# One encoder layer on one core: first rows, gate units, head turns and the first chunks of w_down put in another order

## The chip, the core and the metric

The kernel runs as one program on one core of one Trainium2 chip. The metric is the device time of one execution in microseconds (us); lower is better. The input is one sequence of 512 tokens with 1024 channels, all in float32. Three executions of the kernel before took 872.28, 873.8 and 875.06 us; their median, 873.8 us, is the time that the changed kernel is held against.

## The reference

```python
n = rms_norm(h, mix_norm_g)
proj = n @ w_in                                  # 5120 columns: xa | zu | zv | ga | gb
ya = s5_branch(xa, ...)                          # bidirectional state-space scan, then a GLU
yb = sgu_branch(zu, zv, ...)                     # gating within 128-token chunks
merged = sigmoid(ga) * (ya @ w_proj_a) + sigmoid(gb) * (yb @ w_proj_b)
h = h + merged @ w_out
h = h + memory_cross_attention(rms_norm(h), rms_norm(mem), w_q, w_k, w_v, w_xo)   # 4 heads of 256
h = h + (silu(rms_norm(h) @ w_gate) * (rms_norm(h) @ w_up)) @ w_down              # 2816 wide
return rms_norm(h, final_norm_g)
```

## The kernel before, in words

**Products.** TensorE (PE) is fed float32 numbers as two parts: `split` (L83) copies a tile to a rounded "hi" on ScalarE (ACT, L85) and takes the remainder "lo" on VectorE (DVE, L86). Each product is then three matmuls, hi by hi, hi by lo and lo by hi (`mm3`, L390). A weight tile is 128 x 1024 numbers. It is loaded into one of three `wraw` buffers by SyncE's DMA queue (SP), split into one of three `whi` and three `wlo` buffers, and used. Large products (gates of `b`, queries, feed-forward) are done by a Strassen-Winograd scheme: seven smaller products `q` = 1 to 7 for each "unit" of 512 columns, with sums of operands made by DVE or by accumulating DMAs.

**Order.** The list `plan` (L329 to L362) names every weight tile in the order of use; `next_w` (L365) issues loads some entries ahead and splits up to two entries ahead. `tick` (L485) counts the planned PE time in steps of 5.2 us and starts what `later` (L475) has put down as due; the state-space branch (S5) is a generator, `s5_program`, that `tick` feeds in between. The order in which the lines are traced gives priorities only: when the program is built, a scheduler places each engine's instructions by its own model of their times, so an instruction that it takes to be ready can be hoisted over ones traced before it. At run time each engine works through its queue in the order so fixed. `keep_in_program_order` (`in_order`) pins an instruction against the other pinned ones of its engine; `tc.issue_after(ins)` puts the instructions traced in its block behind `ins` on that engine.

**First rows.** The token tiles are called t = 0 to 3 (128 rows each, `xt`). Each is squared and summed on ACT (L515), its factor is made by two small DVE instructions and one on GpSimd (POOL, L524 to L526), it is scaled on DVE, turned by eight PE transposes (`ptr`, L554) and split into `xn_hi`, `xn_lo`. In `first_rows` (L607) the gain row is spread over the partitions by small matmuls into `pg`; ACT copies it to `g_mix` (L615) and DVE scales tile 0 straight from `pg` (L616). The first use is `tokm(w_in, OFF_V, ...)` (L1095): for each of four weight tiles, six matmuls into the bank `pt` of each of four token tiles; tiles 0 and 1 go token by token as they come, tiles 2 and 3 at the end.

**S5.** `s5_setup` loads `s5_log_step` into a column of `slab` (L684) and takes its exponential on ACT (L726). `s5_kernels(o)` (L832) makes the products `pk` one tick later (L900). `s5_outputs(p)` (L988) copies the states `zh` into `ss` on ACT (L1002, L1003) and makes the products `py` on PE (L1015); the second pass is traced from tick 34 on (L1065). The four 128 x 1024 tiles `gw` of the b gates stand in the place of `zh` (tag `zh`, L1275), so their loads (L242) wait for the copies.

**b's gates.** `ORDER` (L224) is the order of the two units i = 0, 1 of the gate `b`; `gate_step` (L1306) does one product (24 matmuls of 128 x 256).

**Heads.** `scores` (L1491) makes the softmax of a head, `turn_probs` (L1515) turns it by PE transposes `ppt` and splits it, `values` (L1525) makes the head's output: two groups `po` of six matmuls, each in a bank that ACT and DVE then split into `ot_hi`, `ot_lo`. Heads are counted 0 to 3 in the code. `tokm(w_xo, 0, ...)` (L1598) multiplies the outputs by the first half of w_xo: its weight tiles 0 and 1 need heads 0 and 1, tiles 2 and 3 need heads 2 and 3. Head 2 is turned ahead of it, head 3 one tick into it, and the `hook` makes both heads' values after the blocks of tiles 0 and 1.

**w_down.** `plan_units` (L266) and the loop at L1755 hold the order of the ten feed-forward units. In the last one the first two of six chunks of `down_product(dx, 1, ...)` (L1774) stand between products 6 and 7; `x` is copied to `u3` on ACT (L1776) after product 7, and product 4 goes onto the same bank.

Of the kernel before, what the change touches and what calls it, by code (L numbers as in the profile page):

```python
# [17 lines left out]
P = 128  # L18
# [34 lines left out]
def hybrid_layer_kernel(  # L53
# [29 lines left out]
    def split(dst_hi, dst_lo, src):  # L83

        hi = nc.scalar.copy(dst_hi, src)  # L85
        lo = nc.vector.tensor_tensor(dst_lo, src, dst_hi.bitcast(F32), ALU.subtract)  # L86
        if pinned[0]:
            in_order(hi)
            in_order(lo)


    pinned = [False]
# [131 lines left out]
    ORDER = ((1, 0), (2, 0), (5, 0), (6, 0), (1, 1), (7, 0), (2, 1), (5, 1), (6, 1), (3, 0), (7, 1), (4, 0), (4, 1), (3, 1))  # L224
# [41 lines left out]
    def plan_units(units, down):  # L266
# [122 lines left out]

    def mm3(ps, a, b, start, stop, free=False):  # L390

        for i, (x, y) in enumerate(((0, 0), (0, 1), (1, 0))):
            nc.tensor.matmul(ps, a[x], b[y], start=start and i == 0, stop=stop and i == 2, skip_group_check=free)  # L393
# [38 lines left out]
    def tokm(w, c0, act, nk, evac, ntok=NT, last=2, kpt=2, hook=None, cut=None, t0=0):  # L432
# [6 lines left out]
        for wi in range(nw):  # L439
# [4 lines left out]
            if wi < nw - last:  # L444
# [6 lines left out]
                tick(1.3 * ntok)  # L451
        for t in toks:
# [5 lines left out]
            else:  # L458
                tok_block(ps[t], t, held, act, kpt, full, nw == last, True)
# [88 lines left out]
    def to_feat(src, hi, lo, tsl, full=None, skip=None, part=(0, 1), behind=None):  # L548

        for q in part:  # L550
            ps = aux("ptr", (P, 4, P))
            for j in range(4):
                k = 4 * q + j
                tr = nc.tensor.transpose(ps[:, j, :], src[:, k * P:(k + 1) * P], ident)  # L554
                if behind is not None:
                    in_order(tr)
            if q != skip:
                split(hi[:, 4 * q:4 * q + 4, tsl], lo[:, 4 * q:4 * q + 4, tsl], ps)
# [48 lines left out]
    def first_rows():  # L607
# [4 lines left out]
        idles(2)  # L612
        r = rms_factor(row_sums(xt[:, 0, :]))
        for i in range(2):
            in_order(nc.scalar.copy(g_mix[:, HALF[i]], pg[i]))  # L615
            in_order(nc.vector.scalar_tensor_tensor(xt[:, 0, HALF[i]], xt[:, 0, HALF[i]], r, pg[i], ALU.mult, ALU.mult))  # L616
# [12 lines left out]
    for t in range(1, NT):  # L629
        rms_scale(xt[:, t, :], g_mix, xt[:, t, :], ss)  # L630
# [3 lines left out]
        if t == 1:  # L634
            ss3 = row_sums(xt[:, 3, :])
            pinned[0] = False
        if t == 2:
            ss = ss3

# [33 lines left out]
    def s5_setup():  # L673
# [1247 lines left out]
```

## Time and profile before

| what | value |
|---|---|
| executions of the kernel, us | 872.28, 873.8, 875.06 |
| the profiled execution, us | 875.6 |
| its span, first to last instruction, us | 873.8 |
| PE busy, us (share) | 860.3 (98%) |
| DVE busy, us (share) | 648.0 (74%) |
| ACT busy, us (share) | 475.6 (54%) |
| mean granted PE clock | 0.991 |

The profiled execution took 875.6 us, of which 873.8 us lie between its first and its last instruction; 1.8 us lie around them. A busy engine has an instruction in work; as matmuls overlap each other, PE counts as busy also where they come at half their rate. The granted clock says where that is so.

### The profile page before, as it was taken

To read this page: it belongs to the slowest core of one execution; us is meant where nothing else is said; L and a number is where in the kernel's file an instruction comes from. 1 tells how busy PE (TensorE), PEld (TensorE's weight loads), DVE (VectorE), ACT (ScalarE), POOL (GpSimd) and SP (SyncE) were. 2 spreads that over 40 slices of the span, in tenths; PEclk is the share of its full clock that TensorE was granted. 3 is DMA by queue.
4 is the path that set the end of the run, shared out by engine and by line. 5 is a ranking of instruction groups with operands and counts; after the bars stand their busy time and mean duration, and the time that the engine had idled before them with its cause. 6 is when DMAs were issued, how large, how long until landed. Compare 5 with 4: busy or idle time off the path is not lost.

```text
span 873.8 us, 14852 instructions
## 1 busy us (share of the span) xinstructions
PE 860.3 (98%) x5897; PEld 764.8 (88%) x5897; DVE 648.0 (74%) x897; ACT 475.6 (54%) x704; POOL 108.8 (12%) x157
## 2 busy tenths in 40 slices
PE   8999999999999999999999999999999999999996
PEld 6788888878889988889899878999999999888875
DVE  5599679867748768679658656867877778889875
ACT  5453875267436544557547444645545454655663
POOL 1000066100611010110000001001111111000000
PEclk8999999999999999999999999999999999999998
DMA  7457559844647687934688144557799777467672
GB/s 235 121 154 223 115 179 234 203 121 153 173 121 197 162 223 202 287 113 167 204 253 218 54 151 110 145 135 177 173 222 228 201 194 167 135 205 229 197 249 85
DMA packets 110119, 155.40 MB, mean 178 GB/s; under 512 B 8969, under 2 KB 77089, under 8 KB 109986
## 3 DMA queue, kind: packets, MB, share of 16 engines
q1 hardware_dynamic: 91746, 128.27, 45.1%
q0 software_dynamic: 18016, 25.66, 18.5%
q8 instruction: 46, 0.75, 0.3%
q10 hardware_dynamic: 288, 0.52, 0.2%
q14 instruction: 23, 0.19, 0.1%
HBM read 148.70 MB, written 37.20 MB: 213 GB/s over the span
## 4 chain that ended last, share of the span: by engine, by line
PE 95%; DVE 1%; DMA 1%; SPq 1%; ACT 0%; issue 0%; POOLq 0%; POOL 0%; ACTq 0%
PE pf L393 27%; PE pt L393 18%; PE px L1221 12%; PE dx L393 7%; PE pq L1221 6%; PE dq L393 3%; PE pv L1221 3%; PE gx L1221 3%; PE qx L1221 2%; PE dv L393 2%; PE py L1015 1%; DMA slab<-in_s_log_step_dram 1%; PE gq L1221 1%; PE ptr L554 1%; PE po L393 1%; PE qq L1221 1%
## 5 line engine op out<-in xcount | busy, mean ns | idle before, releaser
L86 DVE TENSOR_TENSOR wlo<-wraw,whi 128x1024 fp32r<-128x1024 f32 (+1 forms) x135 | 160.0, 1185 | 82.4 <-ACT whi L85 82.0
L85 ACT CAST whi<-wraw 128x1024 fp32r<-128x1024 f32 (+1 forms) x135 | 138.0, 1023 | 145.0 <-PE pf L393 46.9
L393 PE MATMUL pf<-xn,whi 128*128 128x512 f32 x320 | 100.4, 393 | 0.0
L1221 PE MATMUL px<-fn,whi 128*128 128x256 f32 x480 | 83.3, 276 | 0.0
L1221 PEld LDWEIGHTS px<-fn,whi 128*128 128x128 f32 x480 | 72.5, 188 | 0.3 <-ACT u L1776 0.2
L393 PEld LDWEIGHTS pf<-xn,whi 128*128 128x128 f32 x320 | 59.5, 188 | 12.7 <-issue 0.7
L86 DVE TENSOR_TENSOR wlo<-b,whi 128x1024 fp32r<-128x1024 f32 x40 | 48.9, 1222 | 28.9 <-ACT whi L85 28.9
L85 ACT CAST whi<-b 128x1024 fp32r<-128x1024 f32 x40 | 42.2, 1054 | 51.2 <-PE px L1221 27.1
L1221 PE MATMUL px<-fn,wlo 128*128 128x256 f32 x240 | 66.4, 277 | 0.0
L393 PE MATMUL pf<-xn,wlo 128*128 128x512 f32 x160 | 62.6, 392 | 0.0
L393 PE MATMUL dx<-whi,s 128*128 128x512 f32 x170 | 53.9, 392 | 1.4 <-ACT whi L85 1.0
L1221 PE MATMUL pq<-s,whi 128*128 128x256 f32 x320 | 55.1, 276 | 0.0
L86 DVE TENSOR_TENSOR wlo<-t,whi 128x1024 fp32r<-128x1024 f32 x30 | 36.7, 1224 | 19.9 <-ACT whi L85 19.9
L85 ACT CAST whi<-t 128x1024 fp32r<-128x1024 f32 x30 | 31.6, 1053 | 35.8 <-PE pv L1221 12.6
L1221 PEld LDWEIGHTS pq<-s,whi 128*128 128x128 f32 x320 | 48.3, 188 | 0.1
L393 PE MATMUL pt<-whi,xn 128*128 128x512 f32 x128 | 45.4, 430 | 1.9 <-ACT xn L85 1.9
L1221 PEld LDWEIGHTS px<-fn,wlo 128*128 128x128 f32 x240 | 45.1, 188 | 0.0
L1221 PE MATMUL pq<-s,wlo 128*128 128x256 f32 x160 | 44.2, 277 | 0.0
L393 PEld LDWEIGHTS dx<-whi,s 128*128 128x128 f32 x170 | 31.7, 188 | 8.5 <-ACT whi L85 1.2
L393 PEld LDWEIGHTS pf<-xn,wlo 128*128 128x128 f32 x160 | 30.1, 188 | 6.3 <-issue 0.2
L311 POOL DMA_DIRECT2D dsum<-in_w_down_dram x12 | 13.3, 1108 | 163.3 <-DMA dsum<-in_w_down_dram 163.3
L393 PE MATMUL dx<-wlo,s 128*128 128x512 f32 x85 | 33.1, 390 | 0.0
(478 smaller groups left out, 2342.4 us busy)
## 6 DMA issues: line engine op xcount, KB each, us to landing
wraw<-in_w_in_dram SPq DMA_DIRECT2D x35, 512.0 KB, 5.4
dsum<-in_w_down_dram SPq DMA_DIRECT2D x20, 512.0 KB, 5.7
wraw<-dsum SPq DMA_DIRECT2D x20, 512.0 KB, 3.9
b<-in_w_gate_dram SPq DMA_DIRECT2D x15, 512.0 KB, 4.8
b<-in_w_up_dram SPq DMA_DIRECT2D x15, 512.0 KB, 4.5
wraw<-in_w_down_dram SPq DMA_DIRECT2D x15, 512.0 KB, 4.0
dsum<-in_w_down_dram POOLq DMA_DIRECT2D x10, 512.0 KB, 7.7
dsum<-dsum POOLq DMA_DIRECT2D x10, 512.0 KB, 5.5
```

What stands on the lines that cost most here:

```text
L85: hi = nc.scalar.copy(dst_hi, src)
L86: lo = nc.vector.tensor_tensor(dst_lo, src, dst_hi.bitcast(F32), ALU.subtract)
L311: plan[j + step][1].append((0, lambda d=dst, x=more: nc.gpsimd.dma_start(d, x, accum_op=ALU.add)))
L393: nc.tensor.matmul(ps, a[x], b[y], start=start and i == 0, stop=stop and i == 2, skip_group_check=free)
L554: tr = nc.tensor.transpose(ps[:, j, :], src[:, k * P:(k + 1) * P], ident)
L1015: in_order(nc.tensor.matmul(ps[64 * j:64 * j + 64, :], a, b, start=g % 4 == k == 0, stop=k == 2, tile_position=(0, 64 * j), skip_group_che ...
L1221: nc.tensor.matmul(ps[:, j, :], a[x], b[y], start=start and j == k == i == 0, stop=k == 3 and i == 2, skip_group_check=True)
```

## The change

**First rows.** DVE scales both halves of tile 0 before anything else of `first_rows`; on ACT the hi part of each half of the first weight tile now goes ahead of the copy to `g_mix`; the lo part is pinned behind the lo part of `xn`. Two idle matmul pairs are gone (`idles(2)`). The scaling of tiles 1 to 3 goes behind `xn`'s last lo part, the split of weight tile 2 is traced earlier (its lo part behind tile 1's scaling), and the last `pt` blocks of token tile 0 go behind tile 1's transposes. The exponential of `s5_log_step` goes behind the last hi part of `xn` on ACT, the reduction `rs` (L1136) behind the last lo part on DVE.

**S5 and b.** `pk` of the last two octets is made 1.4 ticks later, not 1; the second pass of `s5_outputs` is traced from tick 36.3; `ORDER` takes products 1 and 2 of both units first.

**Heads.** Head 2 is turned after the first block of w_xo (behind its last matmul), head 3 after the third, values of head 2 after the fifth, of head 3 after the seventh; `tokm` ticks after each block (`fine`).

**w_down.** One chunk stands before product 7 of the last unit, the next one after it.

```diff
-    ORDER = ((1, 0), (2, 0), (5, 0), (6, 0), (1, 1), (7, 0), (2, 1), (5, 1), (6, 1), (3, 0), (7, 1), (4, 0), (4, 1), (3, 1))
+    ORDER = ((1, 0), (1, 1), (2, 0), (2, 1), (5, 0), (6, 0), (5, 1), (7, 0), (6, 1), (3, 0), (7, 1), (4, 0), (4, 1), (3, 1))
...
-            between = [nx[1]] if nx else down[:2]
-            plan.extend([m[5], m[6]] + between + [m[7]] + ([nx[2]] if nx else []) + [m[4], m[3]])
+            between, behind = ([nx[1]], [nx[2]]) if nx else (down[:1], down[1:2])
+            plan.extend([m[5], m[6]] + between + [m[7]] + behind + [m[4], m[3]])
...
+                    if fine:
+                        tick(1.3)
+                if not fine:
+                    tick(1.3 * ntok)
...
-                tok_block(ps[t], t, held, act, kpt, full, nw == last, True)
+                with nullcontext() if behind is None or t > t0 else tc.issue_after(behind):
+                    tok_block(ps[t], t, held, act, kpt, full, nw == last, True)
...
-        idles(2)
         r = rms_factor(row_sums(xt[:, 0, :]))
-        for i in range(2):
-            in_order(nc.scalar.copy(g_mix[:, HALF[i]], pg[i]))
-            in_order(nc.vector.scalar_tensor_tensor(xt[:, 0, HALF[i]], xt[:, 0, HALF[i]], r, pg[i], ALU.mult, ALU.mult))
...
+        for i in range(2):
+            in_order(nc.vector.scalar_tensor_tensor(xt[:, 0, HALF[i]], xt[:, 0, HALF[i]], r, pg[i], ALU.mult, ALU.mult))
         for q in range(2):
-            split(hi[:, q, :], lo[:, q, :], raw[:, q, :])
+            in_order(nc.scalar.copy(hi[:, q, :], raw[:, q, :]))
+            in_order(nc.scalar.copy(g_mix[:, HALF[q]], pg[q]))
             to_feat(xt[:, 0, :], xn_hi, xn_lo, slice(0, P), part=(q,))
+            in_order(nc.vector.tensor_tensor(lo[:, q, :], raw[:, q, :], hi[:, q, :].bitcast(F32), ALU.subtract))
...
-        rms_scale(xt[:, t, :], g_mix, xt[:, t, :], ss)
+        r = rms_factor(ss)
+        with tc.issue_after(turned[1].ins):
+            for i in range(2):
+                scaled = nc.vector.scalar_tensor_tensor(xt[:, t, HALF[i]], xt[:, t, HALF[i]], r, g_mix[:, HALF[i]], ALU.mult, ALU.mult)
...
+            with tc.issue_after(scaled.ins):
+                split_w(2)
+            turned1 = row_tr[0]
...
+        stp = small()
+        with tc.issue_after(last_row[0]):
+            A_.activation(stp, ls, AF.Exp)
...
-        A_.activation(stp, ls, AF.Exp)
...
-        later(1, products)
+        later(1 if o < 2 else 1.4, products)
...
-        while side["now"] < 34:
+        while side["now"] < 36.3:
...
-    tokm(w_in, OFF_V, xn, KD, zv_evac(0))
+    tokm(w_in, OFF_V, xn, KD, zv_evac(0), behind=turned1)
...
-        nc.vector.tensor_reduce(rs, wsr, AX.X, ALU.add)
+        with tc.issue_after(last_row[1]):
+            nc.vector.tensor_reduce(rs, wsr, AX.X, ALU.add)
...
-    turn(2, probs2)
-    later(1, lambda: turn(3, probs3))
+    later(0.2, lambda: turn(2, probs2, last_mm[0].ins))
+    later(0.7, lambda: turn(3, probs3))
+    later(1.2, lambda: values(2, *pts.pop(2)))
+    later(1.7, lambda: values(3, *pts.pop(3)))
...
-    tokm(w_xo, 0, ot, KD, add_evac(0, 1, None), hook=lambda: [values(i, *pts.pop(i)) for i in (2, 3)])
+    tokm(w_xo, 0, ot, KD, add_evac(0, 1, None), fine=True)
...
-            down_product(dx, 1, True, range(2))
+            down_product(dx, 1, True, range(1))
         product(x, u, 7, False, ops)
...
+        else:
+            down_product(dx, 1, True, range(1, 2))
         V.tensor_tensor(u3, q, u3, ALU.subtract)
```

`last_mm`, `turned` and `row_tr` only remember instructions for the `issue_after` blocks; `last_row` holds the hi and lo parts of `xn` made last.

More of the change, by code (lines that the diff above doesn't have):

```diff
@@ L722, in s5_setup @@
         st["c"] = (cr, ci)
-        stp, a, rho, th, n, sn, hs, cs = (small() for _ in range(8))
-        A_.activation(stp, ls, AF.Exp)
+        a, rho, th, n, sn, hs, cs = (small() for _ in range(7))
         V.tensor_tensor(a, lr, stp, ALU.mult)
@@ L1513, in scores, with turn_probs @@
         return prob
-    def turn_probs(hd, prob):
+    def turn_probs(hd, prob, behind=None):
         p_hi = ap_.tile([P, NM, T], F32R, tag="p_hi", name="p_hi", bufs=2)
@@ L1519, in turn_probs @@
             ps = aux("ppt", (P, NT, P))
-            for t in range(NT):
-                nc.tensor.transpose(ps[:, t, :], prob[:, t, mt * P:(mt + 1) * P], ident)
+            with nullcontext() if behind is None else tc.issue_after(behind):
+                for t in range(NT):
+                    nc.tensor.transpose(ps[:, t, :], prob[:, t, mt * P:(mt + 1) * P], ident)
             split(p_hi[:, mt, :], p_lo[:, mt, :], ps.rearrange("p t m -> p (t m)"))
@@ L1541, in hybrid_layer_kernel, with turn @@
     pts = {}
-    def turn(hd, probs):
-        pts[hd] = turn_probs(hd, probs)
+    def turn(hd, probs, behind=None):
+        pts[hd] = turn_probs(hd, probs, behind)
     qx, qq_ = unit_bank("qx"), None
```

16 lines of the change are left out of this document (10 added, 6 removed).

## The prediction

> **What bounds the kernel now.** I read the page first, then PE's waits, the chain, and the timelines of the places named there.
>
> ```profile
> span 873.8 us, 14852 instructions
> PE 860.3 (98%) x5897; PEld 764.8 (88%) x5897; DVE 648.0 (74%) x897; ACT 475.6 (54%) x704; POOL 108.8 (12%) x157
> ```
>
> PE is busy in 860.3 of 873.8 us. The change leaves out only two pairs of idle matmuls, so all it can gain is idle time of PE and time in which PE goes at half clock. From the view of PE's waits (total, times, longest):
>
> ```profile
> PE pt L393 <- ACT xn L85: 1.9, 1, 1.9
> ...
> PE dx L393 <- ACT whi L85: 1.0, 1, 1.0
> PE ppt L1521 <- DVE prob L1512: 0.7, 1, 0.7
> PE pt L393 <- ACT ot_hi L85: 0.7, 1, 0.7
> ...
> ```
>
> These four lie where the change works: xn (first rows), dx behind whi (w_down), ppt and ot_hi (heads); 1.9 + 1.0 + 0.7 + 0.7 = 4.3 us. The clock comes on top. The next rows are the timeline of the opening, then the windows view of line L393 in three stretches (length, PE busy and count, PEld, clock, DMA), then two rows of the chain.
>
> ```profile
> 7.44 1.53 DVE L616 SCALAR_TENSOR_TENSOR xt<-xt,r,pg 128x512 f32<-128x512 f32 x2 [1.75 <-ACT g_mix L615]
> 8.09 0.62 ACT L85 CAST whi<-wraw 128x512 fp32r<-128x512 f32 x1
> 11.74 1.23 DVE L86 TENSOR_TENSOR wlo<-wraw,whi 128x1024 fp32r<-128x1024 f32 x1 [0.24 <-ACT whi L85]
> 13.99 1.41 DVE L541 SCALAR_TENSOR_TENSOR xt<-xt,r,g_mix 128x512 f32<-128x512 f32 x2 [0.67 <-POOL r L526]
> 14.79 1.38 PE L554 MATMUL ptr<-ident,xt 128*128 128x128 f32 x8
> 17.33 0.23 ACT L726 ACTIVATE slab<-slab 128x32 f32<-128x32 f32 x1 [1.82 <-DMA slab<-in_s_log_step_dram]
> 17.47 1.06 ACT L85 CAST xn<-ptr 128x512 fp32r<-128x512 f32 x2
> 18.09 0.50 PE L393 MATMUL pt<-whi,xn 128*128 128x512 f32 x1 [1.91 <-ACT xn L85]
> ...
> 19.50 0.63 PE L393 MATMUL pt<-wlo,xn 128*128 128x512 f32 x1
> ...
> 22.49 0.43 PE L393 MATMUL pt<-wlo,xn 128*128 128x512 f32 x1
> ```
>
> ```profile
> 12.32:15.73 3.41, 2.33 (x8) 1.11 (x7) 1.00 0.91 160
> 15.73:19.14 3.41, 1.05 (x5) 0.88 (x6) 1.00 0.36 55
> 19.14:22.56 3.42, 3.42 (x10) 2.68 (x9) 0.50 1.00 293
> 32.80:36.21 3.41, 1.62 (x5) 0.48 (x3) 1.00 0.00 0
> ```
>
> ```profile
> 18.09 7.15 PE pt L393 x23
> ...
> 46.87 21.59 PE pf L393 x95
> ```
>
> The reader is to see one chain. Tile 1's transposes end at 14.79 + 1.38 = 16.17. Their casts to xn could follow, but ACT's queue holds the exponential (L726) ahead of them, and that waits 1.82 us for a DMA. PE stands still until 18.09. One stretch later the clock is 0.50: from 19.50 to 22.49 there are seven steps, 0.43 us each, where the chain's 95 matmuls take 0.227 each. About eight matmuls lose 0.2 us: 1.6 us. The stretch before a drop held 1.05 us of `pt` matmuls (15.73) or 1.62 (32.80, which is followed by the other drop); the one with 2.33 was followed by full clock. So the wait costs 1.9 us by itself and 1.6 through the clock.
>
> **The change part by part.**
>
> *First rows.* DVE's scaling of tile 0 waited for ACT to leave `pg` (1.75 us, L616). In the new order it goes first, some 0.7 us earlier, so the transposes of tile 0 start at about 7.5. On ACT the hi of the first weight half now heads the queue; its cast at 8.09 did not wait, so the tile had landed by then, and I put it at 7.8. Six copies follow each other (hi, g_mix, xn, twice) at about half a us, so that the hi of weight tile 1 follows at 10.7, in time for its lo. DVE loses: the lo of a weight half stands behind the lo of xn, which needs ACT's xn; by the same durations tile 1's lo (11.74) comes at about 12.05, 0.3 late. The factor's two DVE instructions wait behind it, so the scaling of tile 1 is at 14.3 instead of 13.99, its transposes end at 16.5 and not 16.17. With the exponential moved behind the last xn, ACT is free for the casts, and PE starts on tile 1 at about 16.4: 18.09 - 16.4 = **1.7 us** gained. What is late next is the transposes themselves. Bounds: 0, if another instruction that waits takes the exponential's place, and 1.9 + 0.7 = 2.6, if the earlier scaling of tile 0 comes through whole. I take 1.7, since the DVE chain is made of rows.
>
> *The clock.* PE still has some 1.9 us (14.5 to 16.4) with transposes alone. If a stretch of 3.41 us holds all of it, 1.5 us of `pt` matmuls are left, nearer to 1.62 and 1.05 (drop) than to 2.33 (none). If a stretch ends inside it, as one would at 15.73, the clock holds. Either is about as likely, so of 1.6 us I count half, **0.8**; ends 0 and 1.6. The Trainium skill, page "TensorE: Matmul & The Clock Gate", section "Part 1: The HAM clock gate (the "warmup" mystery)", says that the gate looks at free-running windows of 3413 ns and drops after at least one idle window. This trace agrees on the length (19.14 to 22.56), and the drop came after a window that was not idle, with 1.05 us of matmuls. By the rule taken strictly no wait of 1.9 us drops the clock, this term is 0 and the sum is smaller by 0.8.
>
> *rs, weight tile 2, the transposes of tile 1 ahead of tile 0's last blocks.* These are 0. From 18.09 on PE has 23 matmuls in a row before it needs the transposes of tiles 2 and 3, so these are not what it waits for. The exponential's result is first used much later, on DVE:
>
> ```profile
> 31.37 0.19 DVE L727 TENSOR_TENSOR slab<-slab 128x32 f32<-128x32 f32 x1
> ```
>
> *Heads.* Timeline of PE, then ACT and DVE, around the two waits:
>
> ```profile
> 485.05 0.82 PE L1521 MATMUL ppt<-ident,prob 128*128 128x128 f32 x6
> 486.57 0.59 PE L1521 MATMUL ppt<-ident,prob 128*128 128x128 f32 x2 [0.70 <-DVE prob L1512]
> ...
> 503.25 0.39 PE L393 MATMUL po<-p_hi,vt 128*128 128x512 f32 x1
> 504.31 0.50 PE L393 MATMUL pt<-whi,ot_hi 128*128 128x512 f32 x1 [0.68 <-ACT ot_hi L85]
> ```
>
> ```profile
> 503.67 0.59 ACT L85 CAST ot_hi<-po 128x512 fp32r<-128x512 f32 x1 [0.32 <-PE po L393]
> 504.52 0.68 DVE L86 TENSOR_TENSOR ot_lo<-po,ot_hi 128x512 fp32r<-128x512 f32 x1
> ```
>
> Turning head 2, PE runs out of probabilities. The first six transposes start 0.11 apart, the sixth at 485.60; the seventh starts at 486.57 and not at 485.71, so 0.86 is lost. At 503.25 all eight blocks of tiles 0 and 1 are used up, PE has just made the first `po`, and the next matmul needs its cast: 504.31 - 503.25 - 0.23 = 0.83 lost. The change puts one block (six matmuls, 1.36 us) ahead of the turn, and blocks 6 to 8 beside the four `po` groups. A `po` bank is free 1.6 us after its last matmul (503.63 to 505.20, from these rows), so a block of 1.36 covers all but 0.2. I take 0.86 + 0.83 - 0.2 = **1.5 us**. Bounds: 1.7, and a loss of 4.7 (three bank turnovers of 1.57 in the open) if the groups come back to back.
>
> *w_down.*
>
> ```profile
> 759.11 0.28 PE L1221 MATMUL px<-fn,wlo 128*128 128x256 f32 x1
> 759.31 1.04 ACT L85 CAST whi<-wraw 128x1024 fp32r<-128x1024 f32 x1 [0.71 <-PE px L1221]
> 760.26 0.58 ACT L1776 COPY u<-px 128x512 f32<-128x512 f32 x1
> 760.41 0.74 PE L393 MATMUL dx<-whi,s 128*128 128x512 f32 x2 [1.02 <-ACT whi L85]
> ```
>
> Product 4 must wait until ACT has copied `px` to u3, and ACT first splits the third chunk, whose buffer product 7 has just left. PE loses 760.41 - 759.11 - 0.11 = 1.2 us. After the change twelve matmuls of the second chunk (2.7 us) stand there, longer than cast and copy (1.6), and their split is done while PE is in product 6 and 7. I take **1.1**; ends 0 (the scheduler keeps its order) and 1.2.
>
> *S5 and b.* PE is not idle here:
>
> ```profile
> 248.49 0.36 PE py L1015 x2
> 248.85 11.11 PE pf L393 x48
> ...
> 260.08 5.38 PE py L1015 x94
> ```
>
> Two `py` run alone at 248.49 and take 0.36; in their place in the long piece two take 2 x 5.38/94 = 0.11. So a break in the row costs some 0.25. Tick 36.3 lies behind the place where those two run, so one break goes: **0.3** with the smaller ones of `pk`, between 0 and 0.8. The order of b's products is worth 0: the same 24 matmuls each, as long as the weights are there (last rival).
>
> The sum: 1.7 + 0.8 + 1.5 + 1.1 + 0.3 = 5.4 us. In the profiled execution that is 873.8 - 5.4 = 868.4 of span, with 1.8 around it. The runs' median, 873.8, is 1.8 below the profiled execution's 875.6; I take the sum off the median: **868.4**.
>
> **The rivals.**
>
> *The clock gives nothing.* The stretch over the hole at 14.5 to 16.4 can again hold under 1.62 us of `pt`; then the clock drops as now and its term is 0. Against it: with the stretches where they lie in this profile, the one from 15.73 would hold 2.7 us of them. Time: 873.8 - 4.6 = 869.2. The rule of the Trainium skill's page "TensorE: Matmul & The Clock Gate" quoted above gives the same time, by the other road that the wait never cost any clock.
>
> *The opening's lead is lost in the S5 stretch.*
>
> ```profile
> 44.00:66.00 22.00, 22.00 (x102) 18.24 (x101) 21.82 (x50) 10.80 (x23) 1.34 (x1) 1.00 0.54 148
> ```
>
> From 44 to 66 us DVE is busy 21.82 of 22 (third number). If PE comes 2.5 us earlier and DVE does not, a `wlo` is late and PE waits. The same time results if another instruction takes the exponential's place. Against it: DVE's S5 work is started by PE's transposes, so it moves along, and PE does not wait there now. Time: 873.8 - 1.5 - 1.1 - 0.3 = 870.9.
>
> *The change doesn't do what it says in the heads and in w_down.* The scheduler orders by its own model; without an edge (only head 2's turn has one) it may place `po` and the chunks as before. Against it: the traced places move by whole blocks. Time: 873.8 - 2.5 - 0.3 = 871.0.
>
> *Slower: b's weights come late.* `gw` stands in the place of `zh`. Rows of the views of the tiles `ss` and `gw` (shortest, median and longest in ns, first and last start in us):
>
> ```profile
> L1003 ACT COPY ss<-zh x4: 1969/2000/2048, 189.4 to 208.3; 64x1008 f32<-64x1008 f32 x4
> ```
>
> ```profile
> L242 SPq DMA_DIRECT2D gw<-in_w_in_dram x4: 367/500/508, 210.4 to 211.9; - x4
> DMA to landing us min/median/max: 3.6/5.9/9.3
> ```
>
> The last copy ends at 210.3 and the loads go out at once, 50 us ahead of w_proj_b's end at 260. Should the copies stay behind tick 36.3, in w_proj_b's last blocks (248.85 to 260), four of them (two for each octet, 8 us) would end about 261, a load lands at 267, hi and lo take 2.3 more, and b's first product starts at 269 and not 260: 9 us lost, and 1.6 for the clock, 873.8 - 5.4 + 10.6 = 879.0. It decides once the copies end later than about 260 - 5.9 - 2.3 = 252. They have 42 us of room and move by 2.3 ticks, 12 us, if at all.
>
> **How the numbers follow.** The forecast has 0.45, the rivals in their order 0.15, 0.15, 0.15 and 0.10. A measurement here can tell 0.3%, 2.6 us: faster is below 871.2, slower above 876.4. The forecast and the first rival are faster; of the second and third about half falls on either side of 871.2, so: faster 0.60 + 0.14 = 0.74, same 0.16, slower 0.10. The range goes down to 865.5 (upper ends: 2.6 + 1.6 + 1.7 + 1.2 + 0.8 = 7.9, or 865.9) and up to 874.5, where the second and third rival and some of the heads' 4.7 lie; it leaves out the slow rival.
>
> **What would show it.** First rows: no wait of PE on ACT xn above 0.5 us, tile 1's first `pt` at 16 to 17 us; clock 1.00 or 0.50 in the stretch that follows. Heads: PE's waits on `prob` and `ot_hi` gone. w_down: `dx` on `whi` gone near 759, twelve `dx` between products 7 and 4. b: `py` in one piece, `gw` loads still near 210. The prediction is wrong if waits of a new name sum to over 3 us, above all behind ACT before 50 us or at 260.

## The result

The changed kernel takes 872.14 us (median of 13 runs, 870.96 to 875.69), the kernel before, on the same chip, 874.81 (13 runs, 872.28 to 876.54). The ratio is 0.9974, with a 95% interval of 0.9963 to 0.9986: 2.3 us gained (the two medians by themselves lie 2.7 apart), where 5.4 were forecast. In a second comparison (`after_again`, below) the ratio was 0.9981 (0.9967 to 0.9994). So the direction was right and the size less than half. The time lies in the upper half of the range (865.5 to 874.5); the gain, 0.26%, is a little under the 0.3% at which the chances were cut.

### The profile page after: what moved, and what is told of

It is laid out like the page before. It is cut to its first block, busy times and chain, and to the rows that moved or that the text cites. A ratio compares the mean times of both kernels' runs of the same rounds, so it can differ in the third digit from the quotient of the medians.

```text
span 869.9 us, 14841 instructions
## 1 busy us (share of the span) xinstructions
PE 856.6 (98%) x5893; PEld 762.3 (88%) x5893; DVE 648.1 (75%) x897; ACT 475.0 (55%) x704; POOL 106.2 (12%) x157
## 4 chain that ended last, share of the span: by engine, by line
PE 94%; ACT 2%; DMA 2%; DVE 1%; issue 1%; SPq 0%; POOL 0%; POOLq 0%; ACTq 0%; DVEq 0%
PE pf L396 25%; PE pt L396 18%; PE px L1240 13%; PE dx L396 7%; PE pq L1240 6%; PE dq L396 3%; PE pv L1240 3%; PE gx L1240 3%; PE qx L1240 3%; PE dv L396 2%; PE po L396 1%; PE gq L1240 1%; PE qq L1240 1%; PE py L1033 1%; PE ptr L562 1%; PE psc L396 1%
## 5 line engine op out<-in xcount | busy, mean ns | idle before, releaser
L396 PE MATMUL pf<-xn,whi 128*128 128x512 f32 x320 | 99.8, 392 | 0.0
L396 PEld LDWEIGHTS pf<-xn,whi 128*128 128x128 f32 x320 | 59.6, 188 | 12.5 <-issue 0.5
L396 PE MATMUL pf<-xn,wlo 128*128 128x512 f32 x160 | 62.9, 393 | 0.0
L396 PE MATMUL dx<-whi,s 128*128 128x512 f32 x170 | 53.5, 391 | 0.4 <-DVE h L1870 0.4
L396 PE MATMUL pt<-whi,xn 128*128 128x512 f32 x128 | 43.7, 414 | 0.3 <-ACT xn L85 0.2
L396 PEld LDWEIGHTS dx<-whi,s 128*128 128x128 f32 x170 | 31.8, 188 | 7.4 <-issue 0.8
L312 POOL DMA_DIRECT2D dsum<-in_w_down_dram x12 | 13.3, 1109 | 191.5 <-DMA dsum<-in_w_down_dram 191.5
L396 PEld LDWEIGHTS pf<-xn,wlo 128*128 128x128 f32 x160 | 30.1, 188 | 6.3 <-issue 0.2
L396 PE MATMUL dx<-wlo,s 128*128 128x512 f32 x85 | 33.1, 391 | 0.0
```

Source lines behind the costliest of these rows:

```text
L312: plan[j + step][1].append((0, lambda d=dst, x=more: nc.gpsimd.dma_start(d, x, accum_op=ALU.add)))
L396: last_mm[0] = nc.tensor.matmul(ps, a[x], b[y], start=start and i == 0, stop=stop and i == 2, skip_group_check=free)
```

## The profile after

The profiled execution took 871.72 us, 3.9 less than the profiled execution of before. The page's first lines:

```profile
span 869.9 us, 14841 instructions
PE 856.6 (98%) x5893; PEld 762.3 (88%) x5893; DVE 648.1 (75%) x897; ACT 475.0 (55%) x704; POOL 106.2 (12%) x157
```

PE's waits (total, times, longest):

```profile
PE pf L396 <- ACT yb_hi L85: 1.5, 1, 1.5
PE po L396 <- ACT p_hi L85: 1.1, 1, 1.1
...
PE ptr L562 <- ACT g_mix L630: 0.8, 1, 0.8
...
PE gq L1240 <- DVE u L1253: 0.4, 1, 0.4
...
PE pt L396 <- ACT xn L85: 0.2, 1, 0.2
```

All four waits that the prediction names are gone: xn is down from 1.9 to 0.2, and whi before dx, prob and ot_hi are no longer in the list. In their place stand four of new names, 1.5 + 1.1 + 0.8 + 0.4 = 3.8 us. The prediction's own mark for being wrong was 3 us of these. None of the four existed before. The prediction looked for them before 50 us and at 260; only the 0.8 lies there, the others are at 220, 485 and 289 us. Of the 3.9 us between the two spans 3.7 are PE's busy time (860.3 to 856.6) and 0.2 its idle time (13.5 to 13.3): waits were exchanged for others.

What was to show each step did show. In w_down twelve dx stand between products 7 and 4, and PE goes on without a pause (timeline of PE, first row of the block and first row behind it):

```profile
754.12 0.39 PE L396 MATMUL dx<-wlo,s 128*128 128x512 f32 x1
...
756.39 0.40 PE L1240 MATMUL px<-fn,whi 128*128 128x256 f32 x2
```

The loads of gw still go out near 207 (view of the tile, first and last start), far ahead of b, so the rival that makes the kernel slower is out:

```profile
L243 SPq DMA_DIRECT2D gw<-in_w_in_dram x4: 368/500/510, 206.7 to 208.2; - x4
```

## The experiments

Every kernel below was held against the kernel before on its own chip; ratios are to that, with a 95% interval.

### What one program's executions differ in

`before_again` is the kernel before, unchanged, `after_again` the changed one.

> The kernel before once more, unchanged, to see what two executions of one program differ in. Theory: the clock's windows of 3.41 us lie elsewhere against the program in each execution, so the profile of before (three half-rate windows: 8.90, 19.14 and 36.21) was one of several cases; here one or two half-rate windows in other places, the long piece of pf after the opening up to 2 us earlier than 46.87, and the wait of pt on ACT xn of 1.6 to 1.9 as before. The times give 1.000 with an interval of 0.001 on either side. Rival: the windows are set by the program: the same three within 0.5 us, 46.87 again, and the profile of before is typical.

The times give 1.0002 (0.9990 to 1.0014). The trace holds the finding of this study. ACT's and PE's timelines of this second execution, at the place of the 1.9 us wait:

```profile
15.62 0.23 ACT L726 ACTIVATE slab<-slab 128x32 f32<-128x32 f32 x1 [0.52 <-DMA slab<-in_s_log_step_dram]
```

```profile
16.38 0.50 PE L393 MATMUL pt<-whi,xn 128*128 128x512 f32 x1 [0.22 <-ACT xn L85]
```

In the profile from which I forecast, the exponential's load landed at 17.33 and PE went on at 18.09. Here it lands at 15.62, and PE goes on at 16.38: 0.22 us of wait, as in the changed kernel. Five traces here have this opening, with the exponential at this place of ACT's queue. PE's wait on xn is 1.91 and 0.22 us in the two of before, 1.58 with `heads_only`, and under 0.2 with `down_only` and `no_open`, where the exponential didn't wait at all. So the wait comes in two of the five, and in the other three 0.22 us at most.

The clock differs as well. In the windows view of line L393 (length, PE busy and count, PEld, clock, DMA) this execution has one window at half rate in the opening, not three:

```profile
8.86:12.28 3.42, 2.51 (x6) 2.09 (x7) 0.50 1.04 389
12.28:15.69 3.41, 2.15 (x8) 1.12 (x7) 1.00 0.77 177
15.69:19.10 3.41, 2.72 (x12) 2.25 (x13) 1.00 0.67 157
```

So the rival in the expectation is out, as two of the three are missing. But the theory's reason isn't what these traces show: the windows themselves lie almost alike (edges at 8.86 and 12.28 here, at 8.90 and 12.32 there). What differs is PE's work in them. The window from 15.7 has PE busy for 3.19 us here, with all its work counted, and full rate follows; in the first trace, with the wait, it was 1.50, and half rate followed. `heads_only` has the wait too, 1.74 us in that window, and half rate behind it; `down_only` has neither. In these four the drop behind this window goes with the wait for the DMA, as the prediction had read it; where the wait doesn't come, the drop doesn't either. What all this does to PE shows at one place further on, where each execution needs a new lo part on DVE. PE's timeline of before, and then of `before_again`:

```profile
69.20 0.40 PE L393 MATMUL pt<-wlo,xn 128*128 128x512 f32 x1
```

```profile
66.25 0.50 PE L393 MATMUL pt<-wlo,xn 128*128 128x512 f32 x1 [0.59 <-DVE wlo L86]
```

One program, and 2.95 us between two of its executions by then; and the earlier one waits for DVE there. (At the end 2.0 are left: the span is 871.8, with PE busy for 857.8. Against it the changed kernel's trace gains 1.9 us, 1.2 of them busy time.) The same row of the changed kernel:

```profile
65.65 0.50 PE L396 MATMUL pt<-wlo,xn 128*128 128x512 f32 x1
```

Against the first trace of before the opening gains 3.55 us, against the second 0.60. Five traces of the study have the old first rows (69.20, 66.25, 66.22 with `down_only`, 67.81 with `heads_only`, 67.46 with `no_open`): mean 67.39. Eleven have the new ones (65.28 to 65.89 in nine, 67.21 and 67.25 in two): mean 65.87. That is 1.5 us for the first rows at this place, with 3 us between the traces of the old ones. Where nothing else differs it is less: without the wait and with a start at full rate the old ones have 66.22 and 66.25, the new ones 65.28 to 65.89; with a start at half rate (below, under the clock) the old ones have 67.46, the new ones 67.21 and 67.25. The rest is the two executions with the wait, 69.20 and 67.81.

> The changed kernel once more, beside the two runs that follow. Theory: the new waits are in the order of the queues, not in one execution: PE on ACT yb_hi 1.4 to 2.0 near 218 and on ACT p_hi 1.1 near 483 again, gq on DVE u 0.4; ratio 0.997. Rival: they come and go like the wait on xn in the kernel before: one of them under 0.3 us.

872.55 us, ratio 0.9981. The waits on yb_hi (1.5), p_hi (1.1) and DVE u (0.4) are there again. They belong to the order of the queues.

### The first rows

`exp_only` moves only the exponential, behind the last hi part of xn:

```diff
+        stp = small()
+        with tc.issue_after(last_row[0]):
+            A_.activation(stp, ls, AF.Exp)
...
-        A_.activation(stp, ls, AF.Exp)
```

> Only the exponential is issued later, behind the last xn; all else is the kernel before. Theory: the 1.9 us wait of the first token matmul on ACT xn is the exponential's wait for its DMA, so it goes, tile 1 starts near 16.3 instead of 18.09, and PE is 1.7 to 1.9 us ahead from 20 us on; DVE's queue in b is that of the kernel before, so nothing takes it back at 271: 873.0 us (1.8 under the kernel before, 0.998). Rival: what is won in the opening is lost to a free-running clock or later in S5 whatever the queues are, as in the run with all of the first rows: 874.8, ratio 1.000.

Measured: 874.27 us, ratio 1.0000 (0.9989 to 1.0012): nothing. The wait on xn is gone from the trace, but PE waits at 66 us instead. Here are DVE's and PE's timelines there:

```profile
64.82 1.21 DVE L924 TENSOR_TENSOR ex<-bbr,pw 128x1024 f32<-128x1024 f32 x1
...
66.16 1.21 DVE L86 TENSOR_TENSOR wlo<-wraw,whi 128x1024 fp32r<-128x1024 f32 x1
```

```profile
67.42 0.50 PE L396 MATMUL pt<-wlo,xn 128*128 128x512 f32 x1 [0.60 <-DVE wlo L86]
```

The reader is to see that DVE comes from S5's long row straight into this wlo, and that PE is there first. This is the second rival of the prediction, in the stretch that it named, and it holds for the old order of DVE's queue: `before_again`, `down_only`, `heads_only` and `no_open` have the same wait (0.59 to 0.62). With the new first rows no trace lists it. This is DVE's row in the changed kernel:

```profile
64.38 1.22 DVE L86 TENSOR_TENSOR wlo<-wraw,whi 128x1024 fp32r<-128x1024 f32 x1
```

It ends at 65.60, and PE's matmul follows at 65.65, some 0.1 us late. So DVE still sets the time here, in every trace but the first one of before; the new first rows bring DVE there earlier, and that is what PE gains.

`open_only` is all of the first rows (the hunks of `first_rows`, the loop over tiles 1 to 3, `behind=turned1`, the exponential and `rs`), without S5 and b, heads and w_down.

> Kernel before with the change of the first rows alone. Theory (time follows PE's idle time and its clock, stretch by stretch): the wait on ACT xn of 1.9 us is gone and the first clock drop moves to an earlier place; PE is about 3.7 us ahead at 110 us as in the changed kernel, nothing gives it back, so 3 to 4 us below before where the clock drops once less, 2 us where it does not. Rival (the opening's lead is taken back by VectorE between 44 and 88 us): within 1 us of before.

Measured: 875.65 us, ratio 1.0021 (0.9999 to 1.0043). The first rows alone gain nothing and rather lose. PE waits at 271 us, 200 us behind the last edit. DVE's timeline there, then PE's:

```profile
261.04 1.29 DVE L86 TENSOR_TENSOR yg<-ygt,yg 128x512 fp32r<-128x512 f32 x2 [8.10 <-ACT yg L85]
263.00 1.23 DVE L86 TENSOR_TENSOR gsd<-x,gsd 128x1024 fp32r<-128x1024 f32 x1 [0.66 <-ACT gsd L85]
...
272.26 2.35 DVE L86 TENSOR_TENSOR wlo<-gw,whi 128x1024 fp32r<-128x1024 f32 x2
```

```profile
273.54 0.39 PE L1237 MATMUL gx<-gse,wlo 128*128 128x256 f32 x1 [1.85 <-DVE wlo L86]
```

In the kernel before, both lo parts of yg stand behind gsd, gse and a sum of x. Here they stand ahead of gsd, and two more stand ahead of b's second wlo. Nothing in this place was edited. The compiler orders the queues by its own model of the whole program; that an earlier PE in that model turned DVE's queue here is my reading and not shown.

`open_363` is `open_only` with one line more:

```diff
-        while side["now"] < 34:
+        while side["now"] < 36.3:
```

> All of the first rows plus S5's second outputs at tick 36.3; ORDER, pk, heads and w_down as before. Theory: the first rows alone gained nothing because the planned order of DVE's queue 250 us later shifted (two lo's of yg ahead of gsd and of b's wlo) and PE waited 1.9 us for that wlo; here the two lo's stand behind again, so no wait of gx on DVE wlo above 0.5 us, and 2 us less than with the first rows alone: 873.4. Rival: b's gates are late whenever PE comes earlier, since DVE is the limit there: the wait stays at 1 to 2 us, under wlo or gse, and the time at 875.5.

Measured: 872.31 us, ratio 0.9986 (0.9975 to 0.9998). DVE's timeline is in the old order again, and PE has no wait of gx in its list:

```profile
257.14 1.23 DVE L86 TENSOR_TENSOR gsd<-x,gsd 128x1024 fp32r<-128x1024 f32 x1 [4.21 <-ACT gsd L85]
...
265.20 1.29 DVE L86 TENSOR_TENSOR yg<-ygt,yg 128x512 fp32r<-128x512 f32 x2
266.40 1.22 DVE L86 TENSOR_TENSOR wlo<-gw,whi 128x1024 fp32r<-128x1024 f32 x1
```

So the theory holds and the rival falls: it is the order, not DVE's load. Tick 36.3 is what lets the first rows' lead pass b.

`no_open` is the whole change with these hunks undone.

> The whole change but for the first rows and the exponential, which are as before. Theory: the exponential's wait for its DMA comes in about half of the executions and PE's lead is cut to DVE's at 65, so this is 0.6 to 1.0 us above the whole change: ratio 0.998. The forecast's own price, 2.5 us, would give 0.9998. Rival: the first rows are worth nothing at all: 0.997, as the whole change.

Measured: 874.42 us, ratio 1.0003 (0.9991 to 1.0014), against 0.9981 for the whole change on the same chip. So inside the change the first rows are worth 0.22%, 1.9 us with about 1.5 on either side, between what I expected here and the forecast's 2.5; the rival (nothing) is unlikely.

### S5 and b

`no_pk14` is the changed kernel with one line as it was:

```diff
-        later(1 if o < 2 else 1.4, products)
+        later(1, products)
```

> Changed kernel with the products pk of the last two octets one tick later again, not 1.4. Theory (the 1.4 lets the copies to bd go ahead of the cast to yb_hi on ACT, and they wait for POOL, which waits for a load of gw): the wait of PE on ACT yb_hi near 218 us is gone, 1.6 us below the changed kernel, about 4 us below before. Rival (the order of b's units or the later tick 36.3 makes that wait): it stays, same time as the changed kernel.

Measured: 871.74 us, ratio 0.9962 (0.9948 to 0.9975), and no wait on yb_hi. ACT's timeline in the changed kernel, then POOL's, then ACT's of `no_pk14`:

```profile
214.01 0.36 ACT L899 COPY ks<-pk 128x256 f32<-128x256 f32 x1
218.43 0.61 ACT L861 COPY bd<-bbr 64x128 f32<-64x128 f32 x2 [4.05 <-POOL bd L858]
219.05 0.60 ACT L861 COPY bd<-bbi 64x128 f32<-64x128 f32 x2
219.68 0.62 ACT L85 CAST yb_hi<-zu 128x512 fp32r<-128x512 f32 x1
```

```profile
216.74 1.30 POOL L262 DMA_DIRECT2D gw<-in_w_in_dram  x1 [18.10 <-DMA gw<-in_w_in_dram]
218.08 0.58 POOL L858 MEMSET bd<- 128x256 f32 x2
```

```profile
218.32 0.62 ACT L85 CAST yb_hi<-zu 128x512 fp32r<-128x512 f32 x1 [2.55 <-DVE zu L1218]
218.85 0.36 ACT L899 COPY ks<-pk 128x256 f32<-128x256 f32 x1
219.72 0.61 ACT L861 COPY bd<-bbr 64x128 f32<-64x128 f32 x2 [0.51 <-POOL bd L858]
```

Read it from the end. PE needs yb_hi. Its cast has its zu from DVE at 216.73, but ACT's queue holds the copies to bd ahead of it; these wait 4.05 us for POOL to clear bd; and POOL's queue holds, ahead of that, an accumulating load of gw, which waits 18.10 us for the first load of gw to land. With pk made after 1.4 ticks the compiler put the copies ahead of the cast; with 1 tick they stand behind it, and POOL, no earlier than before, holds up ACT for 0.51 us and PE not at all. The ratio alone doesn't tell this kernel from the changed one (0.9974, 0.9963 to 0.9986); the order of the queue does, and the same order without the wait is there in `mend1` to `mend3`. How long the wait is depends on when gw lands: the traces with pk at 1.4 show 1.5, 1.5, 1.6, 1.7 and 2.0 us, and 0.3 in one (`no_down`) where POOL's load went out 1.5 us earlier.

`no_order` is the changed kernel with the old order of b's products:

```diff
-    ORDER = ((1, 0), (1, 1), (2, 0), (2, 1), (5, 0), (6, 0), (5, 1), (7, 0), (6, 1), (3, 0), (7, 1), (4, 0), (4, 1), (3, 1))
+    ORDER = ((1, 0), (2, 0), (5, 0), (6, 0), (1, 1), (7, 0), (2, 1), (5, 1), (6, 1), (3, 0), (7, 1), (4, 0), (4, 1), (3, 1))
```

> The whole change but for the order of b's products, which is the old one. Theory: the new order costs 0.58 us at 288.7 (product 3 waits for u3) and gains nothing, since at tick 36.3 the queue of DVE is in order without it: the wait of gq on DVE u goes, no wait of gx on wlo comes, 871.6 (0.5 under the whole change). Rival: the new order is what keeps b's weights in time when PE comes 3.5 us earlier: a wait of gx on DVE wlo of 1 to 2 us, 873 to 874. The wait on ACT yb_hi (1.5) stays in either case.

Measured: 872.20 us, ratio 0.9978 (0.9966 to 0.9990); the wait of gq on DVE u is gone, and no wait of gx on wlo comes. In the times the order is worth nothing that can be told; at its place it costs 0.58 us, from two rows of DVE's timeline and one of PE's in the changed kernel:

```profile
287.50 1.23 DVE L86 TENSOR_TENSOR wlo<-gw,whi 128x1024 fp32r<-128x1024 f32 x1 [1.86 <-ACT whi L85]
288.65 0.68 DVE L1253 TENSOR_TENSOR u<-gq,u 128x512 f32<-128x512 f32 x1
```

```profile
289.39 0.39 PE L1240 MATMUL gq<-gsd,whi 128*128 128x256 f32 x1 [0.41 <-DVE u L1253]
```

Product 3 needs u3, and in the new order only product (6, 1) covers the copy and the subtraction behind product (7, 0); a wlo of 1.2 us stands between them on DVE.

### Heads

`heads_only` is the heads' part alone, on the kernel before:

```diff
-    turn(2, probs2)
-    later(1, lambda: turn(3, probs3))
+    later(0.2, lambda: turn(2, probs2, last_mm[0].ins))
+    later(0.7, lambda: turn(3, probs3))
+    later(1.2, lambda: values(2, *pts.pop(2)))
+    later(1.7, lambda: values(3, *pts.pop(3)))
...
-    tokm(w_xo, 0, ot, KD, add_evac(0, 1, None), hook=lambda: [values(i, *pts.pop(i)) for i in (2, 3)])
+    tokm(w_xo, 0, ot, KD, add_evac(0, 1, None), fine=True)
```

The expectations of `heads_only` and `heads_fix` count the heads from 1: their heads 3 and 4 are 2 and 3 of the code, and their head 2 is head 1.

> Kernel before with the turn of heads 3 and 4 between w_xo's token tiles alone. Theory (PE's wait has only moved from prob to p_hi): PE waits about 1.1 us on ACT p_hi at the first po after the scores, the wait on ot_hi is gone, 0.4 us below before. Rival (the 1.5 us of the prediction are there when nothing else is changed): 1.5 us below, with no wait on p_hi.

Measured: 873.60 us, ratio 0.9988 (0.9975 to 1.0002). The time lies between theory and rival, and its interval holds both; the waits decide. Those on prob and ot_hi are gone, and one on p_hi (1.1) is there. In the changed kernel, PE's timeline and then ACT's:

```profile
483.03 0.60 PE L1541 MATMUL ppt<-ident,prob 128*128 128x128 f32 x4
484.75 0.73 PE L396 MATMUL po<-p_hi,vt 128*128 128x512 f32 x2 [1.11 <-ACT p_hi L85]
485.32 0.40 PE L396 MATMUL pt<-whi,ot_hi 128*128 128x512 f32 x1
```

```profile
483.63 0.49 ACT L1527 ACTIVATE prob<-psc,nm 128x256 f32<-128x256 f32 x1
483.99 0.23 ACT L1527 ACTIVATION_READ_ACCUMULATOR prob<-psc,nm 128x1 f32 x1
484.08 1.10 ACT L85 CAST p_hi<-ppt 128x512 fp32r<-128x512 f32 x2
```

The last transposes of head 1 start at 483.03; the next thing in PE's queue is head 1's po, which needs their cast, and that stands behind the exponentials on ACT. In the kernel before, head 2's transposes stood in this gap. The change moved those behind w_xo's first block and left the gap open: 1.28 us lost where 0.86 had been.

`heads_fix` is the changed kernel with head 1's po behind w_xo's first block:

```diff
-    values(1, *pts.pop(1))
+    def values_behind(hd, ins):
+        with tc.issue_after(ins):
+            values(hd, *pts.pop(hd))
+    later(0.2, lambda: values_behind(1, last_mm[0].ins))
     later(0.2, lambda: turn(2, probs2, last_mm[0].ins))
```

> Changed kernel with the values of head 2 put behind the first block of w_xo on PE, so that the block stands ahead of the first po of them. Theory (PE waits for p_hi because that po stands ahead of the block): the wait on ACT p_hi of 1.1 us is gone or below 0.3, 1.0 to 1.3 us below the changed kernel. Rival (ACT and DVE are what limits this stretch, and PE meets them at the next instruction): another wait of about the same size within 5 us, same time as the changed kernel.

Measured: 873.42 us, ratio 0.9983 (0.9969 to 0.9997), a miss: the wait is 0.8 and not gone. The compiler moved the last transposes of head 1 behind that block too, so they stand right ahead of po again. What has to lie between transposes and po is one block more.

`mend2` mends the three queues at once: pk as in `no_pk14`, product (4, 0) of b ahead of (3, 0), and head 1's po behind the second block:

```diff
-    values(1, *pts.pop(1))
     later(0.2, lambda: turn(2, probs2, last_mm[0].ins))
+    later(0.45, lambda: values_behind(1, last_mm[0].ins))
...
-    ... (7, 0), (6, 1), (3, 0), (7, 1), (4, 0), (4, 1), (3, 1))
+    ... (7, 0), (6, 1), (4, 0), (3, 0), (7, 1), (4, 1), (3, 1))
```

> The whole change with three mends: pk one tick later again; the po of head 1 behind the second token block of w_xo and not ahead of the first; product (4, 0) of b ahead of (3, 0). Theory: each of the three new waits is only a matter of what stands ahead in a queue, so the waits on yb_hi (1.5), p_hi (1.1) and gq on u (0.4) all go and nothing of their size comes: 871.74 (the change with pk alone put back) less 1.27 less 0.58 = 869.9, ratio 0.9945. Rival: they move on to the next wait (ot_hi or p_lo for the later po, h or wlo in b): 871 to 872.

Measured: 870.64 us, ratio 0.9962 (0.9947 to 0.9976). All three waits are gone, and one of 1.1 us on ACT whi is new at 296, just behind b. So both theory and rival were right in part.

`mend1` is `mend2` with `ORDER` as the change has it.

> The whole change with pk one tick later again and the po of head 1 behind the second token block of w_xo; b's products in the new order. Theory: the waits on yb_hi and p_hi are gone as in the run with three mends; the wait of gq on DVE u (0.58 lost) is back and the wait of pf on ACT whi at 296 (1.23 lost) is gone, since product (4, 0) is not moved: 870.0, ratio 0.9955. Rival: the wait at 296 doesn't come from (4, 0) but from the earlier PE: 871.2.

Measured: 869.56 us, ratio 0.9936 (0.9923 to 0.9949). The wait at 296 is gone, so it did come from product (4, 0). PE's timeline at the heads:

```profile
482.86 0.60 PE L1541 MATMUL ppt<-ident,prob 128*128 128x128 f32 x4
483.21 0.47 PE L396 MATMUL pt<-whi,ot_hi 128*128 128x512 f32 x1
...
484.68 0.60 PE L1541 MATMUL ppt<-ident,prob 128*128 128x128 f32 x4
485.04 0.72 PE L396 MATMUL po<-p_hi,vt 128*128 128x512 f32 x2
```

Six pt of w_xo's second block now stand in the 2.2 us between head 1's transposes (482.86) and its po (485.04), and PE doesn't stop.

`mend3` is `mend1` with the old `ORDER`.

> As the run before it, with b's products in the old order. Theory: neither the wait on DVE u nor that on whi at 296 is there, and DVE's queue in b stays as in the kernel before because of tick 36.3: 869.5, ratio 0.995, the fastest of all. Rival: with PE earlier still at 271, b's wlo is late: a wait of gx on DVE wlo above 0.5 us, 870.5 to 871.5.

Measured: 869.67 us, ratio 0.9943 (0.9928 to 0.9958): as `mend1`, so the order of b's products decides nothing here either. Both beat both kernels: `mend1` is 0.64% under the kernel before, the whole change 0.26%.

### w_down

`down_only` is w_down's part alone on the kernel before, `no_down` the whole change without it:

```diff
-            between = [nx[1]] if nx else down[:2]
-            plan.extend([m[5], m[6]] + between + [m[7]] + ([nx[2]] if nx else []) + [m[4], m[3]])
+            between, behind = ([nx[1]], [nx[2]]) if nx else (down[:1], down[1:2])
+            plan.extend([m[5], m[6]] + between + [m[7]] + behind + [m[4], m[3]])
...
-            down_product(dx, 1, True, range(2))
+            down_product(dx, 1, True, range(1))
         product(x, u, 7, False, ops)
...
+        else:
+            down_product(dx, 1, True, range(1, 2))
```

> Only w_down's first chunks on two sides of product 7; all else is the kernel before. Theory: the wait of dx on ACT whi near 759 (1.02, with 1.18 lost) goes and nothing else moves: 873.2 (1.1 under the kernel before, 0.9987). Rival: the split, or w_down's own later chunks, wait instead: 874.3.

Measured: 872.44 us, ratio 0.9966 (0.9954 to 0.9978): 3.0 us, more than the 1.2 at its place.

> The whole change but for w_down, which is as before. Theory: 1.18 us are lost again behind ACT whi near 756 and nothing else differs: ratio 0.9983, 1.2 us above the whole change. Rival: w_down's part brings more than its place shows, through what DVE and ACT do later in w_down: 2.5 us above the whole change, ratio 1.000.

Measured: 873.11 us, ratio 0.9991 (0.9977 to 1.0004), with the wait on ACT whi back (1.0 of wait, 1.18 lost). Against the whole change on the same chip that is 0.10%, 0.9 us. From above and below the 1.2 us of the trace are the likeliest price; why the part alone measures 3.0 stays open. Its trace shows nothing else that it changes, and its span, 870.7, lies 1.1 below the 871.8 of `before_again`.

## Why the prediction was wrong

Three steps failed. The term of the heads (1.5) left out what the moved transposes had covered; what is left of it is 0.4. The term of S5 and b (0.3) put `pk` and `ORDER` at next to nothing, and they cost about 2.2. The terms of the opening (1.7 and 0.8) took a wait for a DMA and a clock drop of one execution for every execution's; 1.2 to 1.9 was found for both together.

**First rows, 1.7, and clock, 0.8.** The steps came as written: the exponential behind xn, tile 1's first pt at 16.42 where 16.4 was forecast. The size came out at 1.5 by the rows at 66 us, 1.9 by `no_open` and 1.2 by `open_363` (with tick 36.3), so 0.6 to 1.3 too much. But it was not made of the two things that I had named. The wait on xn came in two executions of five (1.91 and 1.58; 0.22 and twice under 0.2 in the others), and the clock gave nothing. The prediction had the warning in its own text: the profiled execution was 1.8 us above the median of three (0.8 above that of the 13 runs). With one trace at hand, a wait for a DMA and the place of the clock's windows are the first things to suspect of that. Instead I took the whole wait and half of the clock off the median. What the first rows bring in executions without that wait, 0.2 to 1.0 us, is DVE's wlo earlier at 65, which I had counted as a danger and not as a gain. Which of the edits does it is not shown. One candidate is rs, which I had put at 0: in the kernel before, DVE waited 2.47 us for its load ahead of 23.81 (2.10 in `before_again`), and in the changed kernel not at all. And the earlier start of the transposes (7.57; I had put 7.5) was lost at once, as a row of ACT and one of PE show:

```profile
8.42 0.58 ACT L630 COPY g_mix<-pg 128x512 f32<-128x512 f32 x1
9.05 1.11 PE L562 MATMUL ptr<-ident,xt 128*128 128x128 f32 x4 [0.82 <-ACT g_mix L630]
```

The second half of the transposes waited 0.82 us for ACT's copy of the first half of g_mix, which now stands behind the hi of the weights. So the first pt came at 9.82, where `before_again` has 9.77.

**The clock.** The changed kernel has two half-rate windows behind each other; here is the windows view of line L396:

```profile
8.41:11.83 3.42, 1.74 (x3) 1.17 (x4) 0.50 1.04 414
11.83:15.24 3.41, 3.41 (x9) 2.27 (x8) 0.50 0.91 230
15.24:18.66 3.42, 2.71 (x11) 1.72 (x10) 1.00 0.21 44
```

The drops at 19.14 and 36.21 are gone, as hoped, but the first stretch is twice as long. The first window, with all work of the engines (length, PE, PEld, DVE, ACT and POOL busy, clock, DMA), in the changed kernel and in `before_again`:

```profile
8.41:11.83 3.42, 2.51 (x7) 1.87 (x8) 2.11 (x4) 3.42 (x8) 0.00 (x0) 0.50 1.04 414
8.86:12.28 3.42, 3.35 (x11) 2.79 (x11) 3.14 (x6) 3.23 (x7) 0.00 (x0) 0.50 1.04 389
```

PE is idle for 0.9 us in the first, with the wait for g_mix and one of 0.27 for the lo part of the weights, which now stands behind that of xn. Nine traces with the new first rows have this double window, and PE is busy for 2.51 to 2.96 us in the first half of it. In the four with the old ones that show windows it is 3.34 or more, and full rate follows. So the new order of the opening seems to bring the second window itself; no run changes these waits alone, so that stays an inference. The other two traces with the new first rows, `no_pk14` and `mend3`, are at half rate until about 17 us. The clock column says 1.00 there; the matmuls, 0.43 us apart, say otherwise. The 6.83 us of the double window stand against 3.41, 3.41, 6.83 and 10.24 in four traces with the old ones (the fifth, `no_open`, is at half rate until 14), and the term is nil.

**Heads, 1.5.** This is the step that failed most plainly, together with the next. Both waits went, 0.86 + 0.83 as counted, and none of the turnover of banks that I had feared came. But of the first one I asked only what it waits for, not what it covered: PE's work in that gap was moved away, and the next instruction of the queue waited for the same engine, 1.28 us. That leaves 0.4.

**S5 and b, 0.3.** The row of py is in one piece, from 257.14 to 262.6, as forecast; what that brings was not measured alone. But of `pk` I wrote that only "smaller ones" of the breaks go. Made 0.4 ticks later, pk turned the order of ACT's queue, and yb_hi came 1.6 us late; the new ORDER costs 0.58 for u3, where I had written 0 (by the rows of its place; the times can't tell it). Taken with the 0.3 of the break, left as forecast, that is about -1.9 where +0.3 was forecast. My slow rival had the right object, gw behind a queue, and the wrong victim: not b's first product at 260, but POOL's bd, and through it ACT, at 218.

**w_down, 1.1.** Right: 1.18 at its place.

The sum of what was found is 1.5 + 0.4 + 1.2 - 1.9 = 1.2 us, or 1.6 with `no_open`'s 1.9 and 0.9 with `open_363`'s 1.2, against 2.3 and 1.7 measured (each with about 1.1 on either side). What was missing from the forecast is 1.1 in the heads, 2.2 in b and up to 1.3 in the opening. The new waits behind pk and in the heads are shown by the runs that mend them both: 0.9974 becomes 0.9936, and the intervals lie apart. With pk alone put back it is 0.9962, within the noise of either.

`mend1` gains 5.6 us, about the forecast's 5.4. That doesn't make the forecast's sum right: its clock term is nil there as well (the double window is there too), and what was found at the places comes to about 1.5 + 1.7 + 1.2 + 0.3 - 0.6 = 4.1. The rest is open.

## What to carry to other kernels

When the profiled execution lies above the median of the times, what it shows of DMA waits and clock windows is partly its own: take a second look at the same kernel before a term is built on them. When work is moved out of a gap, ask what it had covered there and which instruction is next in that queue. And where a compiler orders the queues, an edit can turn two instructions 200 us away; compare the order of every queue, not only the edited places, and look above all for a copy on ACT that waits for POOL behind a DMA.

## What the runs showed of the hardware

No single number told here which window of 3.41 us goes at half rate. In a half-rate window, PE's busy time with all its work counted sorts the thirteen traces that show one in the opening: 3.34 us or more, and full rate followed (four traces); 2.51 to 2.96, and half rate followed (nine). From full rate, windows with 1.50 us (before, from 15.73) and 1.74 us (`heads_only`, from 15.08) were followed by half rate, one with 2.38 us (`before_again`, from 22.51) by full rate. But the window of before from 32.80 was busy from end to end, and half rate followed; and those ahead of the first half-rate window were busy for 2.85 to 3.29 us, nearly all of it with transposes, idle matmuls and the small matmuls of `pg`. The `pt` matmuls alone, by which the prediction went, don't sort them either: 1.62 us (before, from 32.80) were followed by half rate, 1.30 (`before_again`, from 22.51) by full rate, 2.58 (`open_363`, from 9.78) by half.

The Trainium skill, page "TensorE: Matmul & The Clock Gate", section "Part 1: The HAM clock gate (the "warmup" mystery)", asks for at least one idle window ahead of a drop. The length of the windows that it gives, 3413 ns, agrees with the rows here (3.41 us); but the drops of before at 19.14 and 36.21 came after windows that were not idle, and the measurement decides.

The granted clock of the profile can miss a stretch at half rate: in `no_open`, `exp_only`, `no_pk14` and `mend3` it says 1.00 throughout the opening, while the matmuls of 512 columns come about 0.43 us apart until some time between 13.4 and 17.1 us, and 0.23 us apart later.

The 8 KB loads of s_log_step, sent out at the same point of the program (between 5.1 and 6.3 us), let the exponential go at 15.62, 16.76 and 17.33 us in three executions, and had landed by 15.19 in a fourth: a spread of 2 us.
